# A two-layer hybrid encoder trunk: its opening as one pinned list of steps, and four smaller moves behind it

## The chip, the cores and the metric

The kernel runs on one core of one Trainium2 chip. The metric is the device time of one execution in microseconds (us), lower is better. Five engines work side by side, each on its own list of instructions, which it goes through in order: TensorE (PE, matrix products and their weight loads, PEld), VectorE (DVE), ScalarE (ACT), GpSimd (POOL) and SyncE (SP), which issues the DMAs. Products are written to PSUM, and everything else lies in SBUF or in memory.

## The reference

What is computed, cut to what matters here (batch 1, 1024 tokens, width 1024):

```python
c_act = silu(c)
for layer in (0, 1):
    sh1, sc1, g1, sh2, sc2, g2 = split(c_act @ mod_w[layer] + mod_b[layer], 6)
    h = rms_norm(x, norm_g[layer, 0]) * (1 + sc1) + sh1
    if layer == 0:                      # mixer A, matrix memory, chunked
        q, k, v, o_pre, i_pre, f_pre = split(h @ w_in)
        y = (sigmoid(o_pre) * rms_norm(mlstm(q, k, v, i_pre, f_pre), head_norm)) @ w_out
    else:                               # mixer B, latent attention
        hs = rms_norm(x, kv_norm) * (1 + kv_scale) + kv_shift
        ckv, k_rope = split(hs @ w_dkv)      # 256 + 64 columns
        q = rms_norm(h @ w_qa, q_norm) @ w_qb  # w_qa: 384 columns
        ...
        y = attention @ w_o
    x = x + g1 * rms_norm(y, norm_g[layer, 1])
    h = rms_norm(x, norm_g[layer, 2]) * (1 + sc2) + sh2
    x = x + g2 * rms_norm(relu(h @ w1) ** 2 @ w2, norm_g[layer, 3])
```

## The kernel before

Products are made in three passes on rounded halves: every operand is split into a high part (a cast on ACT, line 118) and a low part (a subtraction on DVE, line 119), and `mm3` (lines 168 to 170) multiplies high by high, and twice high by low. Working tiles come from one pool of 52 SBUF units of a thousand columns. PSUM is cut into two double banks (`MM`) and four single banks (`SM`). Weights pass a queue: `plan` enters them, `_raw` loads the next from HBM, `_split` makes its halves, `take` hands them out, and `ahead` and `early` say how many are kept split and loaded in advance.

The order of work on each engine is not the order of the source. A planner at compile time gives every instruction the source's order as its priority and lets each engine take the first one that it believes ready. Two things bind it: `issue_after(ins)` keeps what is traced inside behind `ins` on that engine, and `behind(PE, V, S)` does the same with the last instruction traced so far on each engine named.

**The opening** (`layer_a`, lines 943 to 1158). The hidden state of the first 512 tokens must be turned (features onto partitions), scaled and shifted before any product can start. Scale and shift are a product of `c_act` with 1024 x 2048 numbers, 8 MB that come in four slabs of 256 features each, with the weights of the first products between them. For a slab, the sum over its eight row blocks is made either by `mod_row` on PE (slab 0: 16 matrix instructions into one row) or by `mod_sum` on DVE (slabs 2, 4, 6: eight instructions of 512 columns, lines 1030 and 1032). `mod_cols` then sums over partitions and turns the result into columns, by one-column products (line 1051) and two DVE instructions (1054, 1055). `turned` does this for a pair of feature blocks and then for each block: four transposes of x on PE (208) into one of the two halves of the double bank `turn`, scale and shift on ACT (985), the split. What PE does in between are `value(k)`, 12 products of 344 columns for the first value and gate columns of four token blocks, into four `SM` banks, and `query(h, k)`, three of 512 columns, into the second double bank `heads`. These calls are nested by hand in `behind` blocks, lines 1112 to 1153.

**Behind the opening**: the second pieces of the values, with the turning of the other 512 tokens between them; values for token blocks 4 to 7 (each `proj_piece` is 24 products of 344 columns); `gates` (line 1295), a generator whose steps turn the gate columns, run a chain of small DVE and ACT instructions on 32 x 128 numbers, and turn results back, between the products of queries and values; `rope_tables` (line 1470), cosine and sine of the positions. `mods`, another generator, makes the remaining rows of shift, scale and gate by `gemv`: each of eight steps per row loads 512 KB and adds one product on DVE (line 292), and later steps turn the row into columns on PE (208) for a write to HBM. Both are stepped by hand between products.

**The mixer's loop** (lines 1204 to 1234) computes the output gate of eight column blocks with ACT's Sigmoid (1231) next to the recurrence's Exp (1406); DVE multiplies by the head norm (1232).

**From the first MLP to attention** (`done0` in `run`, and `latent_*`): when a token block of the MLP is done, `residual` adds it to x; its last addition is put on GpSimd (`self.G`, line 445). `later` then runs the latent projections: `latent_in` norms and turns the block, `latent_mix` multiplies by `w_dkv` (320 columns) and `w_qa` (384). The scale of the norm is folded into these weights when they are split (1542, 1543), and the shift into a bias row: DVE sums shift times weights (1547, 1549), and the split's last part sums it over partitions with a product with ones (1552), copied back by ACT (1553).

Of the kernel before, what the change touches and what calls it, by code (L numbers as in the profile page):

```python
# [65 lines left out]
class Trunk:  # L66
# [186 lines left out]
    def late_consts(self):  # L253

        T = self.T
        self.posi = self.C("posi", [NT, P], I32)
        self.dma(out=self.posi, in_=T["positions"].rearrange("o (b p) -> (o b) p", p=P))
        self.inv = self.C("inv", [P, 32])
        self.dma(out=self.inv, in_=bcast(T["inv_freq"], 32))
        self.gbias = self.C("gbias", [32, 2])  # L260
        gb = T["a_b_gates"]
        for i in range(2):
            self.dma(out=self.gbias[:, i : i + 1], in_=bass.AP(tensor=gb.tensor, offset=gb.offset + i * AH, ap=[[1, AH], [0, NT], [1, 1]]))
        self.kvg = self.C("kvg", [P, KVL])
# [9 lines left out]
        self.headg = self.lcols[:, 8:16]  # L274

# [667 lines left out]
    def layer_a(self):  # L943
# [59 lines left out]

        xs, slabs, sums, accs = [], [], {}, {}

# [12 lines left out]
        def slab_part(k, i):  # L1018

            return slabs[k // 2][i // 2][:, i % 2]  # L1020

        def mod_sum(k, r0=0, r1=KD):

            if r0 == 0:
                accs[k] = self.U("acc")[:, : 4 * P].rearrange("p (s c) -> p s c", s=2)
            acc = accs[k]
            for i in range(r0, r1):
                c = self.cact[:, i : i + 1]
                if i == 0:
                    V.tensor_scalar(out=acc, in0=slab_part(k, i), scalar1=c, scalar2=None, op0=ALU.mult)  # L1030
                else:
                    V.scalar_tensor_tensor(out=acc, in0=slab_part(k, i), scalar=c, in1=acc, op0=ALU.mult, op1=ALU.add)
            for j in range(2):
                sums[k + j] = acc[:, :, j * P : (j + 1) * P]

        def mod_row(k):

            ps = self.SM()
            for i in range(KD):
                PE.matmul(ps[0:1].rearrange("p (s c) -> p s c", s=2), self.cact[:, i : i + 1], slab_part(k, i), start=i == 0, stop=i == KD - 1)  # L1040
            row = self.U("acc")[0:1, : 4 * P]
            S.copy(row, ps[0:1])
            for j in range(2):
                sums[k + j] = row.rearrange("p (s c) -> p s c", s=2)[:, :, j * P : (j + 1) * P]

        def mod_cols(k, ps):

            for j in range(2):
                acc = sums.pop(k + j)
                for s in range(2):  # L1050
                    PE.matmul(ps[:, 2 * s + j : 2 * s + j + 1], acc[:, s], self.ones[: acc.shape[0], 0:1], start=True, stop=True)
            ks = slice(k, k + 2)
# [3 lines left out]

        def turned(k):

            for j in range(2):
                ps = turn[:, j * 512 : j * 512 + 512]  # L1060
                if j == 0:
                    mod_cols(k, turn[:, 512:])
                self.transposes(ps, [x[:, (k + j) * P : (k + j + 1) * P] for x in xs[:4]])
                modulate(k + j, ps, self.U("t")[:, :512], *hT_part(0, k + j, slice(0, 512)), True)

# [31 lines left out]
        with self.tc.issue_after(self.last()):  # L1097
            next(late)
        w, wq, acc = [], [], [None] * 4

        def value(k):
            for tb in range(4):
                if k == 0:
                    acc[tb] = self.SM()
# [3 lines left out]
        def query(h, *ks):  # L1108
            for k in ks:
                c = tuple(u[:, k * P : (k + 1) * P] for u in wq[h])  # L1110
                self.mm3(heads[:, h * 512 : h * 512 + 512], c, self.hT_half(hT, 0, k), k == 0, k == KD - 1)

        normed(xs[:4], 2)
        with self.behind(V, S):
            w.append(self.take(("v", 0, 0)))
            with self.behind(V, S):
                mod_sum(2, 0, 2)
                mod_row(0)
                turn, heads = self.MM(), self.MM()
                with self.behind(V):  # L1120
                    turned(0)
        mod_sum(2, 2)
        wq.append(self.take(("q", 0)))
        value(0)
        with self.behind(PE, V, S):
            turned(2)
        with self.behind(PE, V, S):
            value(1)
            w.append(self.take(("v", 0, 1)))
            wq.append(self.take(("q", 1)))  # L1130
            with self.behind(V):
                mod_sum(4)
            value(2)
            value(3)
        with self.behind(PE, V, S):
            turned(4)
        with self.behind(PE, V, S):
            query(0, 0, 1, 2, 3)
            query(1, 0, 1, 2, 3)
            w.append(self.take(("v", 0, 2)))  # L1140
            with self.behind(V):
                mod_sum(6)
            value(4)
        with self.behind(PE, V, S):
            turned(6)
        with self.behind(PE):
            value(5)
            query(0, 4, 5)
            query(1, 4, 5)
            value(6)  # L1150
            value(7)
            query(0, 6, 7)
            query(1, 6, 7)
        w1 = [self.take(("v", 1, g)) for g in range(3)]
        for tb in range(4):
            values(tb, acc[tb])
        for h in range(2):
            put_qk("q", q, h, 0, heads[:, h * 512 : h * 512 + 512])
        normed(xs[4:], 0)
# [7 lines left out]
        finish(late)  # L1167
        self.ahead, self.early = 3, 3
        self.pump()
# [4 lines left out]
        )  # L1174
        for tb in range(4, NT):
            values(tb, proj_piece(w, tb))
        steps = self.gates(gi, gf)
        next(steps)
        self.rope_tables()

        def mod_steps(n):
            for _ in range(n):
                next(mods, None)

        for h in range(2):
# [25 lines left out]
        for j in range(KD):  # L1211
# [15 lines left out]
            for pr in range(4):  # L1227
                if j % 4 == 0:
                    sg[j // 4][pr] = self.U("sg")
                dst = sg[j // 4][pr][:, :1024].rearrange("p (j t) -> p j t", j=4)[:, j % 4]  # L1230
                S.activation(dst, ps[:, pr * 256 : (pr + 1) * 256], AF.Sigmoid)
                V.tensor_scalar(out=dst, in0=dst, scalar1=self.headg[:, j : j + 1], scalar2=None, op0=ALU.mult)
                if j >= 2:
# [61 lines left out]
    def gates(self, gi, gf):  # L1295
# [38 lines left out]
        yield  # L1334
        yield
        ps = self.SM()
        PE.transpose(ps[:1, 0:32], bl, self.ident[:32, :32])
# [10 lines left out]
        p3 = mr[:, 32:64].rearrange("p (h c) -> p h c", c=NT)  # L1348
        V.tensor_copy(p3[:, :, 1:NT], m3[:, :, 0 : NT - 1])
        yield  # L1350
        ps = self.SM()
# [174 lines left out]
    def plan_latent(self):  # L1526
# [5 lines left out]
        def plan(name, src, n, kg, a, b, o):  # L1532
            for k0 in range(0, KD, kg):
                nk = min(kg, KD - k0)

                def split(hi, lo, raw, k0=k0, nk=nk):
# [3 lines left out]
                    for i in range(nk):  # L1540
# [7 lines left out]
                        else:  # L1548
                            V.scalar_tensor_tensor(out=bias, in0=raw[:, s], scalar=b[:, k : k + 1], in1=bias, op0=ALU.mult, op1=ALU.add)
                    if k0 + nk == KD:  # L1550
                        ps = self.SM()
                        PE.matmul(ps[:, :n], self.ones, bias, start=True, stop=True)
# [15 lines left out]
    def latent_mix(self, t, r, h):  # L1568
# [4 lines left out]
        for dst, w, n, kg, o in ((t, self.wdkv, n, 3, 0), (u, self.wqa, QL, 2, n)):  # L1573
            ps = self.SM()
            for k in range(KD):
                c = (k % kg) * n
                a = tuple(v[:, k * P : (k + 1) * P] for v in h)
                self.mm3(ps[:, :n], a, tuple(v[:, c : c + n] for v in w[k // kg]), k == 0, k == KD - 1)
            self.V.scalar_tensor_tensor(out=dst[:, :n], in0=ps[:, :n], scalar=r, in1=self.lb["bias"][:, o : o + n], op0=ALU.mult, op1=ALU.add)
            yield  # L1580
# [292 lines left out]
    def run(self):  # L1873
# [21 lines left out]
        def done0(tb, y):  # L1895
# [81 lines left out]
```

## Time and profile before

| | us |
|---|---|
| three runs, median (lowest to highest) | 2284.15 (2282.27 to 2289.24) |
| the profiled execution, its own time | 2283.3 |
| its span in the trace | 2281.5 |
| PE busy, with weight loads beside it | 2199.2 and 1833.2 |
| DVE, ACT, POOL busy | 1693.9, 1031.2, 473.2 |
| mean granted clock of PE, share of full speed | 0.991 |

The trace counts from the span's start. A row of the timeline gives start, duration, engine, line, operation, output from input and shape; in brackets stands idle time just before it and what ended that. Products overlap, so the distance from one start to the next is what a product takes on PE; the chain of waits (the work that ended last, in order of time) gives that distance. "sm" is a single bank, "mm" a double bank.

### The profile page before, as it was taken

The page shows a single profiled execution, that of the slowest core. Times are in us where ns is not written, and L with a number is a line of the kernel's source. Part 1 is how long each engine was busy: PE and PEld are TensorE (multiplying, and loading weights), DVE is VectorE, ACT ScalarE, POOL GpSimd, SP SyncE. Part 2 cuts the span into 40 slices and gives each one's busy share as a digit, 9 for nine tenths or more (in the row PEclk, how much of TensorE's full clock was granted, in tenths as well). Part 3 has the DMA queues.
Part 4 walks back from the last instruction along what each step waited for, and adds up shares of the span by engine and source line. Part 5 has one row for each costly group of instructions (what it writes and reads, how often), then busy time and mean ns, then how long its engine had stood idle before and what let it go on. Part 6 is the DMA issues. An engine that isn't in the chain of part 4 may idle for free.

```text
span 2281.5 us, 28823 instructions
## 1 busy us (share of the span) xinstructions
PE 2199.2 (96%) x10746; PEld 1833.2 (80%) x10746; DVE 1693.9 (74%) x2496; ACT 1031.2 (45%) x1708; POOL 473.2 (21%) x317
## 2 busy tenths in 40 slices
PE   6999999999999999999999999999999999999998
PEld 4988888887778877777799989988787888777776
DVE  5577687667987767878978676664678877687888
ACT  3421367564444464333344544555734444633322
POOL 0000110004543333331011000000054433333300
PEclk7999999999999999999999999999999999999999
DMA  8287443234874464454322000022357645545452
GB/s 297 71 271 261 152 131 120 88 107 131 260 237 152 153 196 145 134 171 132 123 75 59 13 17 12 29 84 102 110 158 229 193 141 189 171 134 160 130 173 104
DMA packets 300068, 320.16 MB, mean 140 GB/s; under 512 B 16041, under 2 KB 252185, under 8 KB 299929
## 3 DMA queue, kind: packets, MB, share of 16 engines
q1 hardware_dynamic: 299928, 318.33, 44.2%
q8 instruction: 84, 1.38, 0.2%
q14 instruction: 56, 0.45, 0.1%
HBM read 245.85 MB, written 72.43 MB: 140 GB/s over the span
## 4 chain that ended last, share of the span: by engine, by line
PE 77%; DVE 14%; ACT 3%; issue 3%; DMA 3%; SPq 1%; POOL 0%; DVEq 0%; ACTq 0%; POOLq 0%
PE mm L168 14%; PE mm L169 14%; PE mm L170 14%; PE sm L168 10%; PE sm L170 9%; PE sm L169 9%; PE sm L208 3%; DVE wlo L598 2%; DVE ul L807 2%; DVE y L813 2%; DMA modw<-in_mod_w_dram 1%; DVE x L733 1%; DVE y L879 1%; DVE acc L292 0%; PE mm L1847 0%
## 5 line engine op out<-in xcount | busy, mean ns | idle before, releaser
L168 PE MATMUL mm<-whi,uh 128*128 128x512 f32 x688 | 273.7, 398 | 15.4 <-DVE y L813 15.1
L169 PE MATMUL mm<-wlo,uh 128*128 128x512 f32 x688 | 271.0, 394 | 0.0
L170 PE MATMUL mm<-whi,ul 128*128 128x512 f32 x688 | 270.5, 394 | 0.0
L813 DVE TENSOR_TENSOR y<-y,mm 128x1024 f32<-128x1024 f32 (+1 forms) x161 | 192.6, 1208 | 84.9 <-PE mm L170 84.8
L625 POOL TENSOR_TENSOR tt<-raw,tt 128x512 f32<-128x512 f32 x60 | 113.6, 1893 | 610.2 <-DVE wlo L598 610.2
L168 PE MATMUL sm<-hSh,whi 128*128 128x512 f32 x560 | 221.8, 396 | 9.2 <-DVE x L733 9.2
L169 PE MATMUL sm<-hSl,whi 128*128 128x512 f32 x560 | 220.4, 394 | 0.0
L170 PE MATMUL sm<-hSh,wlo 128*128 128x512 f32 x560 | 219.3, 394 | 0.0
L733 DVE TENSOR_TENSOR x<-x,sm 128x512 f32<-128x512 f32 x198 | 132.3, 682 | 55.9 <-PE sm L170 52.9
L168 PEld LDWEIGHTS mm<-whi,uh 128*128 128x128 f32 x688 | 129.1, 188 | 55.2 <-DVE y L813 22.7
L807 DVE TENSOR_TENSOR ul<-u,uh 128x896 fp32r<-128x896 f32 (+1 forms) x120 | 153.5, 1318 | 24.8 <-ACT uh L801 24.8
L605 POOL TENSOR_TENSOR tt<-raw,raw 128x512 f32<-128x512 f32 x32 | 63.9, 1997 | 488.8 <-ACT x L740 456.9
L801 ACT CAST uh<-u 128x896 fp32r<-128x896 f32 (+1 forms) x120 | 109.6, 948 | 122.1 <-DVE ul L807 114.0
L170 PEld LDWEIGHTS mm<-whi,ul 128*128 128x128 f32 x688 | 129.2, 188 | 30.2
L169 PEld LDWEIGHTS mm<-wlo,uh 128*128 128x128 f32 x688 | 129.2, 188 | 28.9
L598 DVE TENSOR_TENSOR wlo<-raw,whi 128x1024 fp32r<-128x1024 f32 x104 | 147.6, 1420 | 5.6 <-ACT whi L594 5.6
L168 PEld LDWEIGHTS sm<-hSh,whi 128*128 128x128 f32 x560 | 105.1, 188 | 36.7 <-DVE x L733 7.9
L736 ACT ACTIVATE x<-x 128x1024 f32<-128x1024 f32 x64 | 67.8, 1059 | 143.3 <-DVE x L733 143.2
L594 ACT CAST whi<-raw 128x1024 fp32r<-128x1024 f32 x104 | 108.7, 1046 | 43.7 <-DMA raw<-in_ffn_w_dram 21.5
L170 PEld LDWEIGHTS sm<-hSh,wlo 128*128 128x128 f32 x560 | 105.1, 188 | 25.0
L169 PEld LDWEIGHTS sm<-hSl,whi 128*128 128x128 f32 x560 | 105.2, 188 | 24.2
L292 DVE SCALAR_TENSOR_TENSOR acc<-modw,cact,acc 128x1024 f32<-128x1024 f32 x84 | 114.5, 1363 | 5.3 <-DMA modw<-in_mod_w_dram 3.7
(423 smaller groups left out, 5751.9 us busy)
## 6 DMA issues: line engine op xcount, KB each, us to landing
raw<-in_ffn_w_dram SPq DMA_DIRECT2D x144, 512.0 KB
u<-us SPq DMA_DIRECT2D x112, 448.0 KB
us<-x SPq DMA_DIRECT2D x92, 512.0 KB
modw<-in_mod_w_dram SPq DMA_DIRECT2D x80, 512.0 KB
x<-xn SPq DMA_DIRECT2D x24, 512.0 KB
x<-x SPq DMA_DIRECT2D x24, 512.0 KB
x<-in_x_dram SPq DMA_DIRECT2D x16, 512.0 KB
slab<-in_mod_w_dram SPq DMA_DIRECT2D x32, 256.0 KB
```

The lines of the kernel that those rows point to most:

```text
L168: mm(out, a[0], b[0], start=start, stop=False)
L169: mm(out, a[0], b[1], start=False, stop=False)
L170: mm(out, a[1], b[0], start=False, stop=stop)
L208: self.PE.transpose(out[: s.shape[-1], j * P : j * P + s.shape[0]], s, self.ident[: s.shape[0], : s.shape[0]])
L292: self.V.scalar_tensor_tensor(out=acc, in0=t, scalar=self.cact[:, k : k + 1], in1=acc, op0=ALU.mult, op1=ALU.add)
L594: S.copy(x[0], u)
L598: V.tensor_tensor(out=x[1], in0=u, in1=x[0].bitcast(F32), op=ALU.subtract)
L625: G.tensor_tensor(out=t1, in0=b21, in1=t2, op=ALU.subtract)
L733: V.tensor_tensor(out=dst, in0=src, in1=ps, op=ALU.add)
L801: S.copy(x[0], u)
L807: V.tensor_tensor(out=x[1], in0=u, in1=x[0].bitcast(F32), op=ALU.subtract)
L813: V.tensor_tensor(out=dst, in0=dst, in1=ps, op=ALU.add)
```

## The change

1. The opening is one list of steps, and each step stands behind the one before it on PE, DVE and ACT. Transposes (`turn`) are steps of their own, two single banks per pair; scaling and splitting (`made`) follow later in the list. The value sums move into the two double banks, the queries into single banks. Two of the eight row blocks of slab 2 go from DVE to PE; `mod_cols` adds both sums with twice the one-column products.
2. `rope_tables` is traced right behind the turning of the second 512 tokens, before values 4 to 7 (before: behind the first step of the gates); `early` is 2 instead of 3 from there; six steps of `mods` lie behind values 5, 6 and 7 instead of behind the two query products; the gates get two more empty steps, so that more products lie between their parts.
3. The output gate is `(tanh(o/2) + 1) * (head_norm/2)`, the same number, with the half made once.
4. The sum of the latent bias over partitions is made at its first use in `latent_mix`, its product behind the products of the block.
5. `done0` adds the residual on DVE.

The diff, cut to these:

```diff
+        self.headg = self.C("headg", [P, KD])
+        self.V.tensor_scalar(out=self.headg, in0=self.lcols[:, 8:16], scalar1=0.5, scalar2=None, op0=ALU.mult)
...
+        def mod_row(k, r0=0, r1=KD):
+            ps = self.SM()[0:1]
+            for i in range(r0, r1):
+                PE.matmul(ps..., self.cact[:, i : i + 1], slab_part(k, i), start=i == r0, stop=i == r1 - 1)
...
+        def mod_cols(k):
+            ps = self.SM()
             for j in range(2):
                 for s in range(2):
+                    for i, acc in enumerate(sums[k]):
+                        PE.matmul(ps[:, 2 * s + j : 2 * s + j + 1], acc[:, s, j * P : (j + 1) * P], self.ones[...], start=i == 0, ...)
...
+        def turn(*ks):
+            for k in ks:
+                turned[k] = self.SM()
+                self.transposes(turned[k], [x[:, k * P : (k + 1) * P] for x in xs[:4]])
+        def made(k):
+            modulate(k, turned.pop(k), self.U("t")[:, :512], *hT_part(0, k, slice(0, 512)), True)
...
+        both = [self.MM() for _ in range(2)]
+        acc = [both[tb // 2][:, tb % 2 * 512 : tb % 2 * 512 + 512] for tb in range(4)]
...
+        for step in (
+            (mod_row, 0), (mod_cols, 0), (turn, 0, 1), (split_v, 0), (mod_sum, 2, 0, 2), (made, 0), (mod_sum, 2, 2, 4), (made, 1),
+            (value, 0), (mod_row, 2, 6), (value, 1), (mod_sum, 2, 4, 6),
+            (mod_cols, 2), (turn, 2, 3), (split_q, 0), (split_v, 1), (query, 0, 0, 1), (made, 2), (split_q, 1), (made, 3),
+            (value, 2), (mod_sum, 4), (value, 3), (query, 0, 2, 3), (query, 1, 0, 1),
+            (mod_cols, 4), (turn, 4, 5), (split_v, 2), (query, 1, 2, 3), (mod_sum, 6, 0, 3), (made, 4), (mod_sum, 6, 3, 5), (made, 5),
+            (value, 4), (value, 5), (mod_sum, 6, 5), (query, 0, 4, 5),
+            (mod_cols, 6), (turn, 6, 7), (query, 1, 4, 5), (made, 6), (made, 7),
+            (value, 6), (value, 7), (query, 0, 6, 7), (query, 1, 6, 7),
+        ):
+            with self.behind(PE, V, S):
+                step[0](*step[1:])
...
         finish(late)
-        self.ahead, self.early = 3, 3
+        self.rope_tables()
+        self.ahead, self.early = 3, 2
...
         for tb in range(4, NT):
             values(tb, proj_piece(w, tb))
+            if tb > 4:
+                mod_steps(2)
         steps = self.gates(gi, gf)
-        next(steps)
-        self.rope_tables()
         for h in range(2):
+            next(steps)
             put_qk("q", q, h, 1, self.proj_half(self.SM(), wq[h], hT, 1))
-            next(steps)
-            mod_steps(3)
...
-                S.activation(dst, ps[:, pr * 256 : (pr + 1) * 256], AF.Sigmoid)
-                V.tensor_scalar(out=dst, in0=dst, scalar1=self.headg[:, j : j + 1], scalar2=None, op0=ALU.mult)
+                S.activation(dst, ps[:, pr * 256 : (pr + 1) * 256], AF.Tanh, scale=0.5)
+                V.tensor_scalar(out=dst, in0=dst, scalar1=1.0, scalar2=self.headg[:, j : j + 1], op0=ALU.add, op1=ALU.mult)
...
-                    if k0 + nk == KD:
-                        ps = self.SM()
-                        PE.matmul(ps[:, :n], self.ones, bias, start=True, stop=True)
-                        S.copy(bias, ps[:, :n])
...
+            if o not in self.lb:
+                bias = self.lb["bias"][:, o : o + n]
+                total = self.SM()
+                with self.tc.issue_after(self.last()):
+                    self.PE.matmul(total[:, :n], self.ones, bias, start=True, stop=True)
+                self.S.copy(bias, total[:, :n])
+                self.lb[o] = bias
...
-            xn = self.residual(y, st["g"], st["x"].pop(tb), self.G)
+            xn = self.residual(y, st["g"], st["x"].pop(tb))
```

More of the change, by code (lines that the diff above doesn't have):

```diff
@@ L273, in late_consts @@
         self.lcols = yield from self.columns("lcols", 32, vectors, True)
-        self.headg = self.lcols[:, 8:16]
+        self.headg = self.C("headg", [P, KD])
+        self.V.tensor_scalar(out=self.headg, in0=self.lcols[:, 8:16], scalar1=0.5, scalar2=None, op0=ALU.mult)
     def normg(self, l, n):
@@ L1002, in values @@
             put_v(tb, 0, ps, 8, VP - 8)
-        xs, slabs, sums, accs = [], [], {}, {}
+        xs, slabs, sums, turned = [], [], {k: [] for k in range(0, KD, 2)}, {}
         def load_xs(t0, t1):
@@ L1024, in mod_sum @@
             if r0 == 0:
-                accs[k] = self.U("acc")[:, : 4 * P].rearrange("p (s c) -> p s c", s=2)
-            acc = accs[k]
+                sums[k].append(self.U("acc")[:, : 4 * P].rearrange("p (s c) -> p s c", s=2))
+            acc = sums[k][0]
             for i in range(r0, r1):
@@ L1032, in mod_sum @@
                     V.scalar_tensor_tensor(out=acc, in0=slab_part(k, i), scalar=c, in1=acc, op0=ALU.mult, op1=ALU.add)
-            for j in range(2):
-                sums[k + j] = acc[:, :, j * P : (j + 1) * P]
-        def mod_row(k):
-            ps = self.SM()
[L1039 to L1049, printed above, removed]
-                for s in range(2):
-                    PE.matmul(ps[:, 2 * s + j : 2 * s + j + 1], acc[:, s], self.ones[: acc.shape[0], 0:1], start=True, stop=True)
+        def mod_row(k, r0=0, r1=KD):
+            ps = self.SM()[0:1]
+            for i in range(r0, r1):
+                PE.matmul(ps.rearrange("p (s c) -> p s c", s=2), self.cact[:, i : i + 1], slab_part(k, i), start=i == r0, stop=i == r1 - 1)
+            row = self.U("acc")[0:1, : 4 * P]
+            S.copy(row, ps)
+            sums[k].append(row.rearrange("p (s c) -> p s c", s=2))
+        def mod_cols(k):
+            ps = self.SM()
+            for j in range(2):
+                for s in range(2):
+                    for i, acc in enumerate(sums[k]):
+                        PE.matmul(
+                            ps[:, 2 * s + j : 2 * s + j + 1], acc[:, s, j * P : (j + 1) * P], self.ones[: acc.shape[0], 0:1],
+                            start=i == 0, stop=i == len(sums[k]) - 1,
+                        )
+            del sums[k]
             ks = slice(k, k + 2)
@@ L1055, in mod_cols @@
             V.scalar_tensor_tensor(out=a[:, ks], in0=a[:, ks], scalar=1.0, in1=self.normg(0, 0)[:, ks], op0=ALU.add, op1=ALU.mult)
[L1057 to L1064, printed above, removed]
+        def turn(*ks):
[4 more added lines that the diff above has]
+            modulate(k, turned.pop(k), self.U("t")[:, :512], *hT_part(0, k, slice(0, 512)), True)
         q, kT = [None] * 4, [None] * 4
@@ L1098, in layer_a @@
             next(late)
-        w, wq, acc = [], [], [None] * 4
+        w, wq, heads = [], [], []
+        both = [self.MM() for _ in range(2)]
+        acc = [both[tb // 2][:, tb % 2 * 512 : tb % 2 * 512 + 512] for tb in range(4)]
         def value(k):
             for tb in range(4):
-                if k == 0:
-                    acc[tb] = self.SM()
                 o = (k % 3) * VP
@@ L1108, in query @@
         def query(h, *ks):
+            if len(heads) == h:
+                heads.append(self.SM())
             for k in ks:
                 c = tuple(u[:, k * P : (k + 1) * P] for u in wq[h])
-                self.mm3(heads[:, h * 512 : h * 512 + 512], c, self.hT_half(hT, 0, k), k == 0, k == KD - 1)
-        normed(xs[:4], 2)
[L1114 to L1153, printed above, removed]
+                self.mm3(heads[h], c, self.hT_half(hT, 0, k), k == 0, k == KD - 1)
+        def split_v(g):
+            w.append(self.take(("v", 0, g)))
+        def split_q(h):
+            wq.append(self.take(("q", h)))
+        normed(xs[:4], 2)
@@ L1154, in layer_a @@
         w1 = [self.take(("v", 1, g)) for g in range(3)]
+        for h in range(2):
+            put_qk("q", q, h, 0, heads[h])
         for tb in range(4):
             values(tb, acc[tb])
-        for h in range(2):
-            put_qk("q", q, h, 0, heads[:, h * 512 : h * 512 + 512])
         normed(xs[4:], 0)
@@ L1174, in layer_a @@
         )
-        for tb in range(4, NT):
-            values(tb, proj_piece(w, tb))
-        steps = self.gates(gi, gf)
-        next(steps)
-        self.rope_tables()
         def mod_steps(n):
@@ L1183, in mod_steps @@
                 next(mods, None)
+        for tb in range(4, NT):
+            values(tb, proj_piece(w, tb))
+            if tb > 4:
+                mod_steps(2)
+        steps = self.gates(gi, gf)
         for h in range(2):
+            next(steps)
             put_qk("q", q, h, 1, self.proj_half(self.SM(), wq[h], hT, 1))
-            next(steps)
-            mod_steps(3)
         for p in (1, 2):
@@ L1335, in gates @@
         yield
+        yield
         ps = self.SM()
@@ L1349, in gates @@
         V.tensor_copy(p3[:, :, 1:NT], m3[:, :, 0 : NT - 1])
+        yield
         yield
@@ L1578, in latent_mix @@
                 self.mm3(ps[:, :n], a, tuple(v[:, c : c + n] for v in w[k // kg]), k == 0, k == KD - 1)
-            self.V.scalar_tensor_tensor(out=dst[:, :n], in0=ps[:, :n], scalar=r, in1=self.lb["bias"][:, o : o + n], op0=ALU.mult, op1=ALU.add)
+            if o not in self.lb:
[5 more added lines that the diff above has]
+                self.lb[o] = bias
+            self.V.scalar_tensor_tensor(out=dst[:, :n], in0=ps[:, :n], scalar=r, in1=self.lb[o], op0=ALU.mult, op1=ALU.add)
             yield
```

1 line of the change is left out of this document (removed).

## The prediction

> **What bounds the kernel now.** I read the page first, then busy time by stage, then the waits of PE and the chain of waits where PE is not full, then single rows.
>
> ```profile
> span 2281.5 us, 28823 instructions
> PE 2199.2 (96%) x10746; PEld 1833.2 (80%) x10746; DVE 1693.9 (74%) x2496; ACT 1031.2 (45%) x1708; POOL 473.2 (21%) x317
> ```
>
> PE is busy for 2199.2 of 2281.5 us. The change takes no product away, so it can only win back the 82 us in which PE idles and the time in which PE runs at a low clock. The busy time by stretch says where these lie (length, busy time of PE, PEld, DVE, ACT, POOL, then the clock granted to PE):
>
> ```profile
> core 0: us, PE busy (x) PEld busy (x) DVE busy (x) ACT busy (x) POOL busy (x), PEclk, DMA share, GB/s
> 10.20:74.10 63.90, 54.29 (x227) 41.30 (x228) 36.56 (x71) 23.44 (x37) 0.80 (x8) 0.81 0.68 223
> 120.90:147.00 26.10, 20.89 (x115) 19.24 (x114) 20.96 (x40) 6.99 (x16) 0.00 (x0) 0.87 0.78 256
> 147.00:380.00 233.00, 232.78 (x1237) 200.86 (x1236) 172.00 (x289) 95.94 (x230) 19.79 (x15) 1.00 0.58 185
> 380.00:410.00 30.00, 26.09 (x135) 21.27 (x134) 25.77 (x57) 21.01 (x42) 0.00 (x0) 1.00 0.31 102
> 1135.00:1147.00 12.00, 8.06 (x29) 6.19 (x28) 8.79 (x20) 5.51 (x12) 2.19 (x1) 0.72 0.31 109
> ```
>
> Four stretches touch the change. The opening idles for 9.6 us, and its clock of 0.81 costs up to 0.19 x 63.9 = 12.1 us more. The gates' stretch idles for 5.2 us at 0.87 (0.13 x 20.9 = 2.7 us). The end of mixer A idles for 3.9 us at full clock. Where the latent projections begin, PE idles for 3.9 us at 0.72 (0.28 x 8.06 = 2.3 us). Between 147 and 380 PE is full, so nothing done to ACT or DVE there shows.
>
> **The opening.** What PE waits for between 10 and 75 us, and then the chain of waits (start, us until the next piece, engine, output, line), in which the same kind of step appears at both clocks:
>
> ```profile
> PE mm L1051 <- DVE acc L1032: 3.6, 1, 3.6
> PE mm L208 <- ACT t L985: 3.6, 4, 0.9
> ```
> ```profile
> 19.60 1.73 PE sm L1040 x4
> 27.15 0.29 PE sm L168
> 28.29 1.15 PE sm L170 x4
> 37.89 1.22 DVE wlo L119
> 41.12 0.76 DVE acc L1032
> 45.08 1.88 PE mm L1051 x8
> 47.20 1.13 PE mm L208 x4
> 59.77 0.80 PE mm L1051 x8
> 62.34 0.66 PE mm L208 x4
> 70.17 0.32 PE sm L170 x2
> 73.97 0.23 PE mm L170
> ```
>
> A product of 344 columns takes 0.16 us at full and 0.29 at low clock, four transposes 0.66 and 1.13, eight one-column products 0.80 and 1.88; a product of 512 columns takes 0.23. Before, the second four transposes of a pair wait for ACT's scaling of the first, 3.6 us in all; with single banks of their own they need not. I follow the new list from the end of `value(0)`, which is bound as before by slab 0 and its columns: 29.4 in both.
>
> - The two row blocks on PE are four of the instructions that take 1.73; at low clock, by the ratio 1.13/0.66, 2.9: 32.3. `value(1)`, 12 x 0.16 = 1.9: 34.2. The sum over partitions now has 16 one-column products, 1.6: 35.8. The pair's eight transposes, 1.3: 37.1.
> - Now DVE decides. Behind the columns (0.3) the list puts three weight splits of 1.22 and two low halves, priced like the 512-column sum at 0.76: 41.3. The last third of `value(3)` stands behind that (0.6), then 12 query products (2.8): 44.7.
> - `mod_sum(4)` starts on DVE at 41.3, eight times 0.76 = 6.1: 47.4. PE waits 2.7 here; before it waited 3.6 at the same kind of place. This wait is what the list leaves.
> - What is left for PE is twice columns and turning, 2 x (0.8 + 1.3), four values, 7.6, and 30 query products, 6.9: 18.7, and some 0.6 of short waits for DVE: 66.7.
>
> Before, the end is 73.97 + 0.23 = 74.2: **-7.5 us**. Ends: -12 if PE stays at full clock and never waits from 29.4 on, -4 if two more such pieces run at low clock. The DMAs keep their order. Cover behind it: the next products need the remaining value weights, split by an ACT and a DVE that are through a little before PE.
>
> **Gates and rotary tables.** PE's waits from 100 to 150, and rows of DVE's timeline:
>
> ```profile
> PE sm L208 <- DVE acc L292: 2.2, 1, 2.2
> PE sm L1337 <- DVE gate L1328: 2.1, 1, 2.1
> ```
> ```profile
> 109.34 0.20 DVE L1475 CAST posf<-posi 8x128 f32<-8x128 int32 x1
> 115.07 0.33 DVE L1312 TENSOR_SCALAR gate<-sm,gbias 32x128 f32<-32x128 f32 x1
> 124.24 0.15 DVE L1333 TENSOR_TENSOR gate<-gate,gate 32x1 f32<-32x1 f32 x1
> ```
>
> The rotary tables occupy DVE from 109.3 to 115, and the gates' chain follows until 124.4, 9.3 us, with PE's next gate step waiting. In the new order the tables lie under four value pieces of 24 x 0.16 = 3.8 us each, 15 us against under 6, so I cost them at nothing; uncovered they cost 5.7. The chain then starts with the first query product and has two of these (24 x 0.23 = 5.5 each) and two value pieces before PE needs it: 18.6 us of cover for 9.3 plus up to six products of `gemv`, now traced ahead of it. The first `gemv` row also starts earlier, and with it the 2.2. Of 5.2 + 2.7 = 7.9 I take **-5**; ends -8 and +3, if a `gemv` product whose weights are late stands ahead of the chain in DVE's list. `early` at 2 drops one load ahead; with three units split, each worth 48 products of 0.23 = 11 us, nothing waits for it: 0.
>
> **Latent bias.** PE's wait, and two rows of DVE:
>
> ```profile
> PE sm L1552 <- DVE lbias L1549: 3.1, 1, 3.1
> ```
> ```profile
> 1134.99 1.29 DVE L119 TENSOR_TENSOR tbl<-sm,tbh 128x512 fp32r<-128x512 f32 x2 [2.21 <-ACT tbh L118]
> 1142.09 0.61 DVE L1543 SCALAR_TENSOR_TENSOR wlo<-raw,modcol,whi 128x384 fp32r<-128x384 f32 x1
> ```
>
> PE stands 3.1 us for the bias of `w_qa` although the first block's halves are ready at 1136.3 and `w_dkv` is split. With the sum behind the product, PE makes these products first and needs the last split of `w_qa` (1142.7) only after them. The 3.1 go, and most of the 2.3 of clock that follow the pause. What is late next is the second block, through DVE and the residual. **-4.5**; ends -5.5 and 0.
>
> **Residual on DVE.** The groups of the addition on both engines, and a DVE instruction on one column:
>
> ```profile
> L445 POOL TENSOR_TENSOR xn<-xn,x 128x1024 f32<-128x1024 f32 x8 | 19.2, 2399 | 101.5 <-DVE xn L444 82.0 <-DVE rsy L180 10.1 <-issue 5.3
> L445 DVE TENSOR_TENSOR xn<-xn,x 128x1024 f32<-128x1024 f32 x23 | 28.1, 1223 | 0.6
> 1162.21 2.44 POOL L445 TENSOR_TENSOR xn<-xn,x 128x1024 f32<-128x1024 f32 x1 [10.06 <-DVE rsy L180]
> 1162.30 2.37 DVE L182 SCALAR_TENSOR_TENSOR rst<-rsy,rsv 128x1 f32<-128x1 f32 x1
> 1167.31 0.21 DVE L182 SCALAR_TENSOR_TENSOR rst<-rsy,rsv 128x1 f32<-128x1 f32 x1
> ```
>
> DVE gains 8 x 1.22 = 9.8 us of work. But it loses blocks: the one-column instruction takes 0.21, and 2.37 when it starts with an addition on GpSimd. If every addition holds DVE so, up to 8 x 2.2 = 17 us go; if half do, the two cancel. Each block's chain gets 1.2 shorter. I take 0; ends -4 and +5.
>
> **Tanh.** ACT's groups from 260 to 400, and two rows:
>
> ```profile
> L1231 ACT ACT_TABLE_LOAD x7 | 9.0, 1283 | 0.1
> L1406 ACT ACT_TABLE_LOAD x6 | 7.7, 1283 | 1.4 <-DVE rsy L197 1.3
> ```
> ```profile
> 280.15 1.28 ACT L1231 ACT_TABLE_LOAD   x1
> 281.45 1.21 ACT L1231 ACTIVATE sg<-mm 128x256 f32<-128x256 f32 x4
> ```
>
> Sigmoid and Exp change ACT's table 13 times, 16.7 us. No Tanh is in the trace: if it shares a table with Exp all 13 go, if not none. PE is full until 380, so only the last change can count, in a stretch that idles 3.9 us for several reasons: **-0.5**; ends -1.3 and +0.5. [...]
>
> **Sum.** -7.5 - 5 - 4.5 - 0.5 = -17.5 us. The profiled execution took 2283.3, of which 2281.5 is span; that gives 2265.8. It lies 0.85 below the median of the three runs, 2284.15, so against the median I say **2267**.
>
> **Rivals.** *Turns of rows late.* The turning of a `gemv` row into columns stands at a fixed place in PE's list. With PE 12 us earlier by then, PE may come before DVE's last product of the row:
>
> ```profile
> 194.44 1.29 DVE L292 SCALAR_TENSOR_TENSOR acc<-modw,cact,acc 128x1024 f32<-128x1024 f32 x1 [0.47 <-DMA modw<-in_kv_mod_w_dram]
> 196.09 1.04 PE L208 MATMUL sm<-ident,acc 128*128 128x128 f32 x8
> ```
>
> Here 0.4 us lie between them, and DVE itself waited for the DMA. Each miss costs what the one at 139 did: 2.2 of idling and up to 2.7 of clock, 4.9. With all eight rows it is +39, 2267 + 39 = 2306; it decides from the fourth row on, where the gain is gone (17.5/4.9 = 3.6). Against it: in 233 us from 147 on PE idles 0.2, and `gemv` starts earlier too.
>
> *The clock stays low in the opening.* Turning blocks now come eight in a row with 8 to 16 one-column products ahead. If that keeps the clock low for half of the 34 us of work after 29.4, it costs 17 x 0.7 = 12 (a step at low clock is 1.7 times as long, by 1.13/0.66): 2279. At low clock throughout it would be twice that, 2291. For it: 0.81 before. Against: the chain shows 1.13 for four transposes at 47.2 and 0.66 at 62.3, behind a dense run of products, and the list has denser ones. [...]
>
> *The gates keep their stall*, since `gemv` products wait ahead of the chain: the term is 0 to +3, 2272 to 2275.
>
> **Numbers.** Forecast 0.60 (2254 to 2271); gates keep their stall 0.14; clock low in the opening 0.16; rows late 0.10. About 0.3%, 6.9 us, is what a measurement of this kernel can tell, so faster means under 2277.3. The first two cases are faster, the third counts as the same, the fourth as slower except where few rows miss (0.02, half faster, half the same): faster 0.75, same 0.17, slower 0.08. The range goes from 2254 (opening -12, gates -8, latent -5.5, residual -4) to 2282, which holds most of the clock's case and leaves the late rows out.
>
> **What would show it.** Right: the last query product of the opening ends near 67 with a mean clock above 0.85; one PE wait of 2 to 3 us for `mod_sum(4)`; no wait at 1337 and none over 1 us on L292; no PE wait for lbias; one table load or none between Tanh and Exp; no L445 on GpSimd. Wrong: an opening that ends after 71; waits of PE for `acc` between 135 and 260; PE idle over 5 us between the last MLP products and the first heads, with DVE full.

## The result, and the profile after

The changed kernel takes 2261.64 us (median; 2261.18 to 2262.2), beside 2285.48 for the kernel before (2282.27 to 2289.24): a ratio of 0.9895, 95% interval 0.9878 to 0.9912. It is 23.8 us faster; the forecast was 17.5 us, 2267, and its range held the time. The head of the page after:

```profile
span 2259.4 us, 28800 instructions
PE 2194.6 (97%) x10758; PEld 1827.5 (81%) x10758; DVE 1687.6 (75%) x2503; ACT 1013.6 (45%) x1695; POOL 459.0 (20%) x309
```

PE's busy time fell by 4.6 us although it has 12 products more; the rest of the gain is idle time. Busy time by stretch, in the columns known from before:

```profile
core 0: us, PE busy (x) PEld busy (x) DVE busy (x) ACT busy (x) POOL busy (x), PEclk, DMA share, GB/s
10.20:66.90 56.70, 52.13 (x258) 38.66 (x258) 33.94 (x66) 22.45 (x36) 0.56 (x8) 0.97 0.76 250
120.90:147.00 26.10, 26.10 (x154) 23.44 (x154) 18.98 (x31) 6.76 (x17) 0.00 (x0) 1.00 0.67 223
147.00:360.00 213.00, 213.00 (x1134) 183.46 (x1134) 161.49 (x280) 78.19 (x211) 21.36 (x15) 1.00 0.59 179
360.00:390.00 30.00, 29.46 (x152) 24.10 (x151) 25.60 (x57) 18.35 (x38) 0.00 (x0) 1.00 0.47 144
1112.00:1124.00 12.00, 12.00 (x67) 10.40 (x66) 9.07 (x15) 2.85 (x8) 0.00 (x0) 1.00 0.65 229
```

The opening idles for 4.6 us at a clock of 0.97 (before: 9.6 at 0.81). The gates' stretch and the first latent block are full (before: 5.2 and 3.9 us idle). The end of mixer A idles for 0.5 instead of 3.9 us, which was not forecast. Now the waits of PE from 10 to 150 us (engine, line, what it waited for: total, times, longest), of which these count:

```profile
PE sm L208 <- DVE posf L1462: 1.8, 1, 1.8
PE sm L1050 <- DVE acc L1033: 1.6, 1, 1.6
PE mm L168 <- ACT hTh L118: 1.1, 1, 1.1
```

The second is the forecast wait for `mod_sum(4)`. The first is new: PE waits with the turning of the positions for DVE's cast of them. The chain of waits in the opening, with the same kinds of step as before:

```profile
26.68 1.81 PE sm L1039 x4
30.57 2.28 PE sm L1050 x16
32.85 0.60 PE sm L208 x4
37.84 0.49 DVE acc L1031
43.98 1.02 PE sm L1050 x8
45.00 0.93 PE sm L208 x8
46.33 0.43 PE sm L169
54.05 0.79 PE sm L1050 x8
54.84 0.93 PE sm L208 x8
```

The two row blocks take 1.81, not 2.9: the clock is high (1.00 from 20 to 40 us). It is low once, behind the wait that ends at 43.98 (a product of 512 columns takes 0.43 at 46.33). Landmarks, before and after, place the gain: the first transposes behind the opening start at 85.35 and 74.94 (10.4 us earlier), the first state product of mixer A at 280.7 and 266.2 (14.5), the last at 385.4 and 366.8 (18.6), the last latent products at 1234.1 and 1210.1 (24.0). On the way to the end 1.9 are given back: the span is 22.1 shorter. Most of the 1.9 is clock: from 1490 to 1510 us it is 0.91 here, which costs 0.09 x 20 = 1.8, and the kernel before has no low clock near there (1.00 from 1250 to 1640 us).

### The profile page after: what moved, and what is told of

It is laid out like the page before. It is cut to its first block, busy times and chain, and to the rows that moved or that the text cites. A ratio compares the mean times of both kernels' runs of the same rounds, so it can differ in the third digit from the quotient of the medians.

```text
span 2259.4 us, 28800 instructions
## 1 busy us (share of the span) xinstructions
PE 2194.6 (97%) x10758; PEld 1827.5 (81%) x10758; DVE 1687.6 (75%) x2503; ACT 1013.6 (45%) x1695; POOL 459.0 (20%) x309
## 4 chain that ended last, share of the span: by engine, by line
PE 78%; DVE 12%; ACT 3%; DMA 3%; issue 3%; SPq 0%; DVEq 0%; POOL 0%; ACTq 0%; POOLq 0%
PE mm L168 14%; PE mm L170 14%; PE mm L169 14%; PE sm L168 10%; PE sm L169 10%; PE sm L170 10%; PE sm L208 3%; DVE wlo L599 2%; DVE ul L808 2%; DMA modw<-in_mod_w_dram 2%; DVE y L814 2%; DVE x L734 1%; PE sm L1420 1%; PE mm L1836 1%; PE mm L1835 0%
```

## The experiments

Each kernel is the changed one but for the edit shown. The kernel before, run beside them, had medians of 2285.72, 2286.37 and 2285.34, and 2285.48 beside the changed kernel, so the base moved by 1 us at most from one round to the next. One kernel's own executions spread by 1 to 8 us, so a difference of 1 us between two medians is within the noise, and one of 2 us is near it.

**old_opening.** All of part 1 undone.

```diff
-        for step in ((mod_row, 0), (mod_cols, 0), (turn, 0, 1), ...):
-            with self.behind(PE, V, S):
-                step[0](*step[1:])
+        with self.behind(V, S):
+            w.append(self.take(("v", 0, 0)))
...
```

> The opening as before, all else as in the changed kernel. Theory A (each part is worth the step by which its landmarks moved in the trace): the first transposes behind the opening moved by 10.6 us, so the time is about 2261.6 + 10.6 = 2272, and PE's clock between 25 and 55 us is about 0.5 to 0.75 again. Rival B (the parts are worth what was forecast, and the rest comes from elsewhere): 2261.6 + 7.5 = 2269. Rival C (PE is full for 230 us behind the opening and the transfers of gemv rows set its pace, so that part of an earlier start is lost): under 2266.

2268.29: +6.65, close to B. PE waits at the same two places of the opening as in the kernel before (3.6 us each there):

```profile
PE mm L1052 <- DVE acc L1033: 5.4, 2, 5.1
PE mm L208 <- ACT t L986: 3.5, 4, 0.9
```

Its first transposes behind the opening start at 81.32, 6.4 us behind the changed kernel's, and 4.0 before those of the profiled execution of before, which ran the same opening. Most of that difference is clock: 0.91 from 10 to 70 us here, 0.80 there, although PE, sooner through its products, waits longer for DVE's sums here (5.4 instead of 3.6). So of the 10.4 us between the two profiles 6.4 belong to the list, and 4.0 to what one execution of the same list has over another.

**unpinned.** The list without its chain.

```diff
-            with self.behind(PE, V, S):
-                step[0](*step[1:])
+            step[0](*step[1:])
```

> The opening's list is traced in the same order, with the same banks and the same split of the sums, but no step is pinned behind the one before it on PE, DVE and ACT. If the pinned order makes the gain, most of the opening's 10.6 us are lost: 2268 or more. Rival (the single banks and the order of tracing make it, and the planner finds the same order by itself): within 1.5 us of 2261.6.

2268.26: +6.6. With the same banks and the same order of tracing, the planner makes another order. The scaling of x comes late on ACT, and PE waits 5.3 us for it before the first turn:

```profile
27.71 0.69 PE L208 MATMUL sm<-ident,x 128*128 128x128 f32 x2 [5.28 <-ACT x L978]
```

The transposes behind the opening start at 86.61, 11.7 us late: later than with the old, hand-nested opening. The pinned order makes this gain; the banks alone do not.

**sum_on_dve.** All eight row blocks of slab 2 on DVE.

```diff
-            (value, 0), (mod_row, 2, 6), (value, 1), (mod_sum, 2, 4, 6),
+            (value, 0), (value, 1), (mod_sum, 2, 4),
```

> All eight row blocks of slab 2 are summed on DVE again, all else as in the changed kernel. If the two blocks on PE are what keeps PE's clock at full speed from 25 to 40 us (PE has less to do and waits longer without them), the clock there falls to about 0.5 to 0.75 and the time grows by 3 us or more: 2265 or more. Rival (DVE has room for 2 x 0.76 us and PE's clock does not hang on it): within 1 us of 2261.6.

2257.86: 3.8 us shorter, against both expectations. The row blocks do not keep the clock up (from 20 to 30 us it is 0.83 here, 1.00 in the changed kernel, and again 0.83 in the run rope_later below, which has them too), and they do not pay: they cost PE four products (1.81 us) and the longer sum over partitions (in the changed kernel 16 one-column products take 2.28, the eight for the next slab 1.02) to spare DVE 2 x 0.76. The transposes behind the opening come 0.6 us earlier (74.33), and the first state product 2.5 (263.7). Each of the two executions has two stretches of low clock by then (0.83 from 20 to 30 and from 40 to 50 us here; 0.83 from 40 to 50 and 0.84 from 80 to 90 in the changed kernel's), so about 2.5 us are the edit's by these two profiles. This execution is the fastest of its four, 6.2 us under the profiled one of the changed kernel; of the rest 3.6 is clock, 1.00 here and 0.94 and 0.91 there, from 650 to 680 and from 1490 to 1510 us (the rows of the changed kernel stand under old_bias).

**old_gates.** All of part 2 undone.

```diff
-        self.rope_tables()
-        self.ahead, self.early = 3, 2
+        self.ahead, self.early = 3, 3
...
-            if tb > 4:
-                mod_steps(2)
...
+            mod_steps(3)
```

> Rotary tables, early loads, mod steps and the gates' empty steps as before, all else as in the changed kernel. Theory A: PE waits again for the gates' chain, but not for the turned positions, so +4: 2265.6. Rival B (forecast): +5, 2266.6. Rival D (the wait for the turned positions, 1.8 us and the low clock behind it, took back most of what this part won): within 1 us of the changed kernel, 2261 to 2263.

2271.35: +9.7, twice what either theory said. PE waits again for the row (2.2) and the gate (2.1), and the first state product starts 6.5 us later (272.7). Another 3.7 us are lost between the first and the last state product (377.0; 104.3 us apart instead of 100.6), where the output gate is tanh and no table changes. So what was won at the end of mixer A comes from part 2. Two more runs split it.

**mods_behind_queries.** Only the rows' six steps go back.

```diff
         for tb in range(4, NT):
             values(tb, proj_piece(w, tb))
-            if tb > 4:
-                mod_steps(2)
...
             put_qk("q", q, h, 1, self.proj_half(self.SM(), wq[h], hT, 1))
+            mod_steps(3)
```

> The six steps of the rows lie behind the two query products again, not behind values 5 to 7, all else as in the changed kernel. If the gates' stretch was won by the earlier start of the rows: PE waits for acc (2.2 us) and for the gate (2.1 us) come back and the first state product is 5 us later, 2266. Rival (the place of the rotary tables and the empty steps of the gates won it): within 1.5 us of 2261.6, no wait for the gate.

2265.58: +3.9. One wait of PE, new against the changed kernel, is the cause; the first state product comes 5.4 us later (271.6):

```profile
PE sm L208 <- DVE acc L293: 4.8, 1, 4.8
```

The turning of the first row stands at a fixed place in PE's list, and the row is not summed by then. The wait for the gate stays away. The rows' earlier start is what the gates' stretch needed; the tables' new place and the empty steps, which no run parts, took the gate's wait away (it is not the number of loads: the next run has three, and no such wait either).

**early_three.** One number.

```diff
-        self.ahead, self.early = 3, 2
+        self.ahead, self.early = 3, 3
```

> Three loads ahead instead of two from the rotary tables on, all else as in the changed kernel. If the number of loads ahead sets the order of DVE at the end of mixer A (there the kernel with all of part 2 undone lost 3.7 us between the first and the last state product): 2265 to 2266, with the wait of PE for the gated block (gt) at 1.9 us again. Rival (forecast: nothing waits for that load): 2261 to 2262.

2263.65: +2.0 by the medians, between the two expectations, and +4.1 in the profiled execution, the slowest of its four. The waits of 1.9 and 0.8 at the end of mixer A are back. PE's timeline there, first in this run, then in the changed kernel (start, duration, line, output from input):

```profile
370.56 0.39 PE L170 MATMUL mm<-hTh,wlo 128*128 128x512 f32 x1
370.79 0.60 PE L1420 MATMUL sm<-Cst,nw 128*128 128x258 f32 x2
372.52 1.97 PE L208 MATMUL sm<-ident,hn 128*128 128x128 f32 x16 [0.78 <-ACT num L1422]
376.39 1.25 PE L208 MATMUL sm<-ident,hn 128*128 128x128 f32 x8 [1.91 <-DVE gt L1452]
```
```profile
366.56 0.60 PE L1420 MATMUL sm<-Cst,nw 128*128 128x258 f32 x2
367.35 0.40 PE L170 MATMUL mm<-hTh,wlo 128*128 128x512 f32 x1
370.82 0.40 PE L170 MATMUL mm<-hTh,wlo 128*128 128x512 f32 x1
371.06 2.35 PE L208 MATMUL sm<-ident,hn 128*128 128x128 f32 x20
```

With three loads ahead, the last output-gate products ("mm<-hTh,wlo") stand ahead of the last state products ("sm<-Cst,nw"), and nothing lies beside the chain that follows these on ACT and DVE. With two, the planner has the state products first, and 16 gate products, 3.7 us, lie beside that chain. Why a load less turns the two around was not traced through the planner.

**rope_later.** The rotary tables one block later.

```diff
-        self.rope_tables()
         self.ahead, self.early = 3, 2
...
+            if tb == 4:
+                self.rope_tables()
```

> The rotary tables are traced behind the values of token block 4 instead of ahead of them, all else as in the changed kernel. If the new PE wait of 1.8 us for the turned positions and the low clock behind it (85 to 90 us) cost time that is not given back, this kernel is 2 to 4 us shorter: 2258 to 2260. Rival: DVE's list is late there for another reason (the halves of the second 512 tokens), or the gates' chain gets late for it; then it is within 1 us, or longer.

2257.82: 3.8 us shorter. The wait for the positions is 0.5 instead of 1.8 us, and no low clock follows it (1.00 from 80 to 120 us). In the profiled execution the first state product comes only 0.4 us earlier (265.7), because its opening has one stretch of low clock more, 1.7 us (the last section); how the 3.8 of the medians are made up was not traced further.

**old_sigmoid.** Part 3 undone.

```diff
-                S.activation(dst, ps[:, pr * 256 : (pr + 1) * 256], AF.Tanh, scale=0.5)
-                V.tensor_scalar(out=dst, in0=dst, scalar1=1.0, scalar2=self.headg[:, j : j + 1], ...)
+                S.activation(dst, ps[:, pr * 256 : (pr + 1) * 256], AF.Sigmoid)
+                V.tensor_scalar(out=dst, in0=dst, scalar1=self.headg[:, j : j + 1], scalar2=None, op0=ALU.mult)
```

> Sigmoid and the whole head norm as before, all else as in the changed kernel. Theory A: the 13 changes of ACT's table come back, and the tail of mixer A from 370 to 410 us idles again by some 3.5 us: +4, 2265.6. Rival B (forecast: only the last change of the table can count): +0.5, 2262.1. Rival E (the tail shrank because the heads' order changed with the earlier opening): the table changes come back in the profile, but PE's idle time from 370 to 410 stays under 1 us.

2256.67: 5.0 us shorter, against all three. ACT's groups from 255 to 410 us show the table changes back:

```profile
L1215 ACT ACT_TABLE_LOAD x7 | 9.0, 1283 | 0.1
L1392 ACT ACT_TABLE_LOAD x6 | 7.7, 1283 | 1.5 <-DVE rst L196 1.4
```

These are 13 loads of 1.28 us, and the changed kernel has none at these two lines. They cost little: from the first to the last state product it is 101.2 us (263.7 to 364.9), 0.6 more than with tanh in these two executions, and the end of mixer A stays full. The part of the gain that can be placed lies ahead of that: the first state product comes 2.4 us earlier, and the wait for the positions is 0.4. What is gone there is the instruction that halves the head norm. The profiled execution, the fastest of its four, is 5.9 us shorter; behind mixer A 3.6 of these are clock, 1.00 from 650 to 680 and from 1490 to 1510 us, where the changed kernel's has 0.94 and 0.91.

**halved_late.** Tanh stays; that instruction moves from the late constants to just ahead of the mixer's loop.

```diff
-        self.headg = self.C("headg", [P, KD])
-        self.V.tensor_scalar(out=self.headg, in0=self.lcols[:, 8:16], scalar1=0.5, ...)
...
         finish(mods)
+        self.headg = self.C("headg", [P, KD])
+        V.tensor_scalar(out=self.headg, in0=self.lcols[:, 8:16], scalar1=0.5, ...)
```

> The tanh gate stays; only the one small DVE instruction that halves the head norm moves from the late constants to the start of the mixer's loop. Theory H (the run with Sigmoid was shorter because this instruction was gone: it stands on DVE ahead of the cast of the positions, for whose turning PE waits 1.8 us, and a low clock follows): PE's wait falls to 0.4 us, and the time is that of the run with Sigmoid, 2256 to 2258. Rival I (Sigmoid itself or its table changes shift ACT's order for the better): the time stays near 2261.6.

2259.09: 2.55 us shorter, 1 us above the expected range. DVE and PE in the changed kernel (timeline), then in this one:

```profile
83.94 0.19 DVE L250 COPY lcols<-sm 128x32 f32<-128x32 f32 x1
84.64 0.81 DVE L988 TENSOR_SCALAR t<-sm,modcol 128x512 f32<-128x512 f32 x1
85.37 0.16 DVE L275 TENSOR_SCALAR headg<-lcols 128x8 f32<-128x8 f32 x1
85.44 0.21 DVE L1462 CAST posf<-posi 8x128 f32<-8x128 int32 x1
85.70 0.22 PE L208 MATMUL sm<-ident,posf 8*128 8x8 f32 x1 [1.80 <-DVE posf L1462]
87.54 0.49 PE L170 MATMUL sm<-whi,hTl 128*128 128x344 f32 x1
```
```profile
84.95 0.19 DVE L250 COPY lcols<-sm 128x32 f32<-128x32 f32 x1
85.06 0.20 DVE L1462 CAST posf<-posi 8x128 f32<-8x128 int32 x1
85.32 0.22 PE L208 MATMUL sm<-ident,posf 8*128 8x8 f32 x1 [0.41 <-DVE posf L1462]
```

The halving takes 0.16 us. But `behind(V)` pins the cast of the positions behind the last DVE instruction traced, which is the halving; that was put behind a scaling of 0.81, and PE's next product in its list is the turning of the positions. Moved, PE waits 0.4, and no product runs at 0.49 there. So the cause of the wait is shown; 1.4 us of wait and, in six profiled runs of eight, 1.7 of low clock behind it make 2.7, near the 2.55 measured. The 2.4 us by which the run with Sigmoid is still shorter arise behind mixer A (the last state products start at 364.9 and 364.7). In the profiled executions most of it goes with the clock: behind mixer A the slowest product of 512 columns ("sm<-hSh,whi") takes 0.63 us here, as in the changed kernel, and 0.50 with Sigmoid, and from the last score product in a single bank ("sm<-krh,qrs") to the first product of the attention's output ("mm<-whi,oTh") it is 11.1 us here (1491.8 to 1502.9) and 9.7 with Sigmoid (1490.5 to 1500.2). That the medians differ for the same reason is not shown.

**old_bias.** Part 4 undone.

```diff
+                    if k0 + nk == KD:
+                        ps = self.SM()
+                        PE.matmul(ps[:, :n], self.ones, bias, start=True, stop=True)
+                        S.copy(bias, ps[:, :n])
...
```

> The latent bias is summed over partitions when the weights are split, as before, all else as in the changed kernel. Theory A: of the 5.5 us won around the first latent block, some 4.5 are from here: 2266.1, with one PE wait of 3 us for the bias. Rival F (the second block's chain with the residual on DVE is what was won): under +1.5, 2263, with the wait of 3 us still there but hidden later by a wait that gets shorter.

2268.48: +6.8, and the wait is there again (1110 to 1150 us):

```profile
PE sm L1539 <- DVE lbias L1536: 3.0, 1, 3.0
```

In the profiled execution, the fastest of its five, the last latent products come 4.4 us late (1214.5), which is theory A; at the end 2.7 are left. But this execution has full clock at two places where the changed kernel's has a stretch of low clock; first this run, then the changed kernel:

```profile
650.00:680.00 30.00, 26.36 (x118) 21.02 (x117) 27.27 (x30) 11.38 (x14) 14.07 (x8) 1.00 0.54 175
1490.00:1510.00 20.00, 16.11 (x117) 14.14 (x116) 16.55 (x33) 14.70 (x34) 0.00 (x0) 1.00 0.34 106
```
```profile
650.00:680.00 30.00, 26.36 (x112) 21.05 (x111) 25.86 (x27) 11.00 (x13) 12.82 (x8) 0.94 0.49 158
1490.00:1510.00 20.00, 16.87 (x103) 14.84 (x102) 14.29 (x28) 12.05 (x27) 0.00 (x0) 0.91 0.33 107
```

Each is worth 1.8 us (0.06 x 30, 0.09 x 20). With both counted in, the part is worth some 6 us in the profiles too, near the 6.8 of the medians: 3.0 of wait, 1.7 of low clock behind it (0.98 from 1050 to 1135 us, 0.02 x 85), and a rest that was not traced.

**old_residual.** Part 5 undone.

```diff
-            xn = self.residual(y, st["g"], st["x"].pop(tb))
+            xn = self.residual(y, st["g"], st["x"].pop(tb), self.G)
```

> The residual of the first MLP's blocks is added on GpSimd as before, all else as in the changed kernel. Theory A: about 1 us of the 5.5 us won around the latent projections is from here: 2262.6. Rival B (forecast: 9.8 us of work against blocked DVE instructions, net nothing): 2261.6, within 0.5. Rival F (most of the 5.5 us is from here): 2265 or more.

2262.51: +0.9. That is nearest to theory A, but the executions overlap (2261.5 to 2263.96 here, 2261.18 to 2262.2 in the changed kernel), so A and B are not told apart; F is out. From 1050 to 1250 us DVE is busier without the eight additions than with them; first this run, then the changed kernel:

```profile
1050.00:1250.00 200.00, 193.88 (x1090) 171.86 (x1089) 174.54 (x416) 84.12 (x212) 25.62 (x24) 1.00 0.26 82
```
```profile
1050.00:1250.00 200.00, 195.59 (x1105) 173.58 (x1103) 171.61 (x427) 85.40 (x215) 8.74 (x16) 1.00 0.26 82
```

2.9 us more busy time with 9.8 us less work (eight additions of 1.22) makes 12.7 us by which DVE's other instructions took longer, 1.6 per addition on GpSimd: an estimate from these rows. One case stands in the timelines, first this run, then the changed kernel:

```profile
1130.95 2.59 POOL L446 TENSOR_TENSOR xn<-xn,x 128x1024 f32<-128x1024 f32 x1 [1.62 <-DVE xn L445]
1131.72 2.90 DVE L808 TENSOR_TENSOR ul<-u,uh 128x1024 fp32r<-128x1024 f32 x1
```
```profile
1131.33 1.22 DVE L808 TENSOR_TENSOR ul<-u,uh 128x1024 fp32r<-128x1024 f32 x1
```

The same subtraction on DVE takes 2.90 us when it starts within an addition on GpSimd, and 1.22 without one.

**halved_late_sum_on_dve.** Both edits together.

> The halving at the loop's start and all eight row blocks of slab 2 summed on DVE. Theory H, and the sum of the two single effects (4 to 5 us and 3.8 us) if they are independent: 2253 to 2254. Rival (both only made a low clock after a pause less likely, and are one effect): 2256 to 2257.

2253.89 (2251.78 to 2255.26), a ratio of 0.9863 to the kernel before, interval 0.9847 to 0.9878: 7.75 us under the changed kernel, and 1.4 more than the 2.55 and 3.8 of the single edits. It is the shortest of all that ran, and beats both kernels.

## Why the prediction was right, and where not

The direction held, and so did the mechanisms of the opening, the gates and the bias; the term for tanh had the wrong sign. The named signs came out: the opening's last query product ends at 66.9, at a mean clock of 0.97, PE waits once for `mod_sum(4)` (1.6 us, less than the 2 to 3 named), there is no wait for the gate, the row or the bias, and no L445 addition on GpSimd for these blocks. By its terms:

| term | forecast | undone alone, by the medians |
|---|---|---|
| opening | -7.5 | -6.65 |
| gates, tables, rows, early | -5 | -9.7 |
| latent bias | -4.5 | -6.8 |
| residual on DVE | 0 | -0.9 |
| tanh | -0.5 | +5.0 |

These add up to -19.1; 4.7 us of the measured 23.8 belong to no part alone. That -19.1 lies so near the forecast -17.5 is in part luck: gates, bias and residual are worth 7.9 us more than forecast, and tanh and the opening 6.4 us less.

- *Opening.* The size is right, and the end too (66.9 for 66.7), but the end by two errors that cancel. The two row blocks ran at full clock, so `mod_sum(4)` ended at 43.98 instead of 47.4, and the wait was 1.6, not 2.7. Behind it PE took 22.9 us instead of 19.3, since some 24 products of the next piece (0.16 each, 3.8 us) were already done by the last query product. And 74.2 was the end of an execution at a clock of 0.80: of the 10.4 us between the profiles only 6.4 are the list's.
- *Clock stays low (rival).* It did not: up to eight transposes in a row beside one-column products, and 0.97.
- *Gates.* The term was too small for two reasons that the runs show. The rows' earlier start was priced at the 2.2 us seen; by its run it is worth 3.9. And "`early` at 2 ... nothing waits for it: 0" failed: that edit is worth 2.0 (4.1 in the profile), through the order of PE's list some 280 us later. The working asked who waits for the load, not what the planner reorders. The other 3.8 of the 9.7 are left for the tables' place and the empty steps, which no run undid alone.
- *Rotary tables.* "I cost them at nothing" failed for the step's first instruction. The tables lie under the value products as said, but the turning of the positions is an instruction on PE, and it waits 1.8 us for DVE.
- *Tanh.* The term failed: the part costs 5.0 us. The table changes are worth 0.6 in the profiles, as forecast: all 13 loads are gone, and none is left between tanh and exp. The halving, which the working did not price, cost 2.55. The other 2.4 go mostly with the clock behind mixer A in the profiled executions.
- *Latent bias.* The wait and the low clock behind it are what was forecast (3.0 and 1.7). The part is worth 6.8 by the medians and some 6 by the profiles with the clock counted in, more than its end of 5.5; where the rest lies is open.
- *Turns of rows late (rival).* It did not happen in the changed kernel; the run with the steps moved back shows its price once, 4.8.

## What to carry to other kernels

Price a moved step by its first instruction on the full engine, and ask what that one waits for: 0.16 us on DVE cost 2.55 us here, because a pin put PE's next product behind it. Where a planner sets the order, a count of loads or an extra small instruction is an edit of the order too, so compare each engine's list far behind the edit. And test the parts of a change by undoing each: here two details of the change, the early halving and the two row blocks on PE, held back part of what the rest won.

## What the runs showed of the hardware

The same list of instructions gets different clocks in different executions. The opening is the same list in the changed kernel and in the one with the later tables. Yet from 20 to 30 us the second gets 0.83 instead of 1.00, and PE gets through 33 instead of 43 instructions; from 80 to 90 us, behind the wait for the positions that only the first has, it is the other way round. Busy time by stretch, first the changed kernel, then the other:

```profile
20.00:30.00 10.00, 7.84 (x43) 5.52 (x43) 6.69 (x11) 5.70 (x9) 0.00 (x0) 1.00 1.12 331
80.00:90.00 10.00, 8.20 (x48) 7.88 (x47) 8.63 (x25) 7.21 (x12) 0.41 (x4) 0.84 0.76 214
```
```profile
20.00:30.00 10.00, 7.84 (x33) 4.44 (x32) 6.69 (x11) 4.22 (x6) 0.00 (x0) 0.83 1.13 331
80.00:90.00 10.00, 9.72 (x64) 9.22 (x64) 7.50 (x13) 8.66 (x15) 0.14 (x2) 1.00 0.53 141
```

A stretch of low clock lasted 3.4 us in three places of the changed kernel that show one whole (45.9 to 49.3, 86.7 to 90.1 and 663.7 to 667.1, at a mean clock of 0.51, 0.52 and 0.50): at half speed it costs 1.7, which is the 0.83 of a 10 us window. The wait of 1.8 us for the positions was followed by one in six of the eight profiled runs that have this wait (in old_opening and sum_on_dve the clock behind it is 1.00), and in none of the four where it is 0.4 to 0.5. The third stands behind a pause of 3.6 us, and the stretch at 1500 us behind one of 2.5. The runs with Sigmoid, with the old bias and with all sums of slab 2 on DVE have waits of the same lengths there (8.9 to 9.2 us in all for "x" ahead of the products of hSh, 8.9 in the changed kernel; one of 2.4 or 2.5 for "pTl") and no low clock behind them: their slowest products "sm<-hSh,whi" and "sm<-pTl,vh" take 0.50 and 0.38 to 0.39 us, the changed kernel's 0.63 and 0.58. So a pause cost its length here and, behind some of these pauses, 1.7 us more; the nine executions of before beside old_opening went from 2280.81 at a mean clock of 0.993 to 2288.32 at 0.989.

What starts a stretch of low clock is not shown. The pauses ahead of the first two were 1.6 and 1.8 us, 1.9 us of transposes lie ahead of the second, and no run here varied the transposes alone.
